# Gate and up products of a SwiGLU encoder on one core: plain tile products against 2x2x2 block products with seven multiplications, with one pool of 4 KB buffers

## The chip, the core and the metric

The kernel runs on one core of a Trainium2 chip. A core has a matrix engine (TensorE, PE in the profile; PEld is its weight loading), VectorE (DVE), ScalarE (ACT), GpSimd (POOL) and SyncE (SP), which here only issues DMA transfers. Each engine works through its own queue in order and waits for others by semaphores. Data lie in SBUF (128 partitions); products of TensorE go to PSUM, eight banks of 128 x 512 float32. The metric is the device time of one execution in microseconds, lower is better.

## The reference

Two layers, each a half-step FFN, a mixer (two attentions and a pooling branch with gates) and a second half-step FFN. The sequence has 512 tokens, the model 1,024 features, the FFN 2,816. The part that matters:

```python
def swiglu(h, w_gate, w_up, w_down):
    return (jax.nn.silu(h @ w_gate) * (h @ w_up)) @ w_down

for l in range(DEPTH):                       # DEPTH = 2
    mod = (c_act @ w_ada[l] + b_ada[l]).reshape(B, N_MOD, D_MODEL)
    h = modulate(rms_norm(x, norm_gain[l, 0]), mod[:, 0], mod[:, 1])
    x = x + 0.5 * mod[:, 2][:, None, :] * swiglu(h, ffn_w_gate[l, 0], ffn_w_up[l, 0], ffn_w_down[l, 0])
    h = modulate(rms_norm(x, norm_gain[l, 1]), mod[:, 3], mod[:, 4])
    x = x + mod[:, 5][:, None, :] * hybrid_mixer(h, ...)
    h = modulate(rms_norm(x, norm_gain[l, 2]), mod[:, 6], mod[:, 7])
    x = x + 0.5 * mod[:, 8][:, None, :] * swiglu(h, ffn_w_gate[l, 1], ffn_w_up[l, 1], ffn_w_down[l, 1])
```

All is float32.

## The kernel before

**Products in two parts.** Activations lie transposed, features on the partitions and the 512 tokens along the free side. Every large operand is kept as a high part rounded to the fast float32 format of TensorE and a low part, the rest. A product then is three matmuls, high by high, low by high and high by low, which accumulate in one PSUM bank (`triple`, L117). Weights come from DRAM in chunks of 128 x 1,024 (4 KB a partition): `wchunk` (L237) issues the load on SyncE into a `raw` buffer, ScalarE copies the high part into `whi` (L262), VectorE subtracts for the low part into `wlo` (L264); while the attentions run GpSimd does that subtraction.

**An FFN** (`Ffn.run`, L459) has 22 feature tiles of 128, in two parts of 12 and 10 tiles. For each tile a gate chunk and an up chunk of eight 128 x 128 blocks are loaded, each is multiplied by h (`hhi`, `hlo`: eight blocks of 128 x 512) in 24 matmuls of 512 columns (`unit`, L445), and `act` (L450) makes SiLU on ScalarE, the product on VectorE and the split in two parts. After a part `k_outer` (L373) multiplies by the down weights, chunk by chunk, into four banks for each half of the 1,024 model features, and `residual_tail` (L413) adds the result to x on VectorE. In the last pass of an FFN, and of the mixer, `k_outer` works in two halves of 256 tokens.

**Between the phases** the next phase's norm is prepared: `Norm.sq` (L299) squares x on ScalarE and adds on GpSimd into `ssum`, and scales x; `Norm.front` (L319) brings the sum to TensorE and VectorE works out the inverse root; `Norm.back` (L333) broadcasts it by a matmul (L345) and works through eight pieces (`piece`, L350): a multiplication on VectorE or GpSimd (`ON_DVE`, L427), the shift and the high part on ScalarE (L358), the low part on VectorE (L359). The two halves of the tokens go one after the other, and the first three units of an FFN are multiplied half by half behind them. Their weights were loaded ahead (`prefetch_weights`, L442) into spare buffers.

**Beside it** 144 vectors of the modulation are worked out (`mod_step`, L190: a load of 512 KB and one multiply-and-sum on VectorE, L196); 128 of them wait in a queue, and `wchunk` takes one for every chunk while an FFN runs and the queue lasts.

**Order.** The program is written with small delayed tasks (`later`, `poll`, counted in units of TensorE's work), and a scheduler then fixes the order on each engine and the buffers. Buffers are named by tags with a count each: `raw` 2, `whi` and `wlo` 3 each, `b` 17, `ptb` 2 of 8 KB, `pta` 1, `v2` and `xv` 4 each; PSUM has four banks named `mm` and four named `acc`.

Of the kernel before, what the change touches and what calls it, by code (L numbers as in the profile page):

```python
# [15 lines left out]
F32 = mybir.dt.float32  # L16
F32R = mybir.dt.float32r
# [12 lines left out]
H = 8  # L30
# [10 lines left out]
def encoder_kernel(tc, xT, c, w_ada, b_ada, gains, w_gate, w_up, w_down, w_qkv, w_f, w_ubg,  # L41
# [16 lines left out]
    NB, NRAW = 17, 2  # L58
# [14 lines left out]
    def blk(tag, dt=F32R):  # L73
        bufs = {"xv": 4, "v2": 4, "b": NB}[tag]
        return st([P, 2, T], dt, tag, bufs)
# [93 lines left out]
    hhi = cp.tile([P, KD, T], F32R, name="hhi")  # L169
    hlo = cp.tile([P, KD, T], F32R, name="hlo")  # L170
# [19 lines left out]
    def mod_step(l, j, d, tag="raw"):  # L190
        raw = st([P, D], F32, tag, {"v2": 4, "raw": NRAW}[tag])
# [28 lines left out]
    MOD_RATE = 1.0  # L220
# [16 lines left out]
    def wchunk(src, shape, side=True, spare=None, lo_eng=None):  # L237
        if lo_eng is None:
            lo_share[1] += 1
            lo_eng = nc.gpsimd if lo_share[0] and lo_share[1] % lo_share[0] == 0 else nc.vector  # L240
# [4 lines left out]
        elif side and in_ffn[0] and mod_tag[0] == "v2":  # L245
            mod_credit[0] += MOD_RATE
            while mod_credit[0] >= 1.0:
                mod_credit[0] -= 1.0
                mod_pop()
        raw = st([P] + list(shape), F32, "raw", NRAW)  # L250
        last["dma"] = nc.sync.dma_start(raw, src).ins
        if spare == "ptb":
            both = st([P, 2] + list(shape), F32R, "ptb", 2)
            hi, lo = both[:, 0], both[:, 1]
        elif spare == "b":
            hi = st([P] + list(shape), F32R, "b", NB)
            lo = st([P] + list(shape), F32R, "b", NB)
        else:
            hi = st([P] + list(shape), F32R, "whi", 3)
            lo = st([P] + list(shape), F32R, "wlo", 3)  # L260
        with behind("scalar"):
            nc.scalar.copy(hi, raw)  # L262
        with behind("vector"):
            lo_eng.tensor_tensor(lo, raw, hi.bitcast(F32), op=ALU.subtract)  # L264
# [23 lines left out]
    class Norm:  # L288


        def __init__(self, l, s, xtag):
            self.l, self.s, self.xtag = l, s, xtag
            self.ssum = st([P, T], F32, "ssum", 1)
# [5 lines left out]
        def sq(self, d, hs):  # L299
# [4 lines left out]
            if d == 0:  # L304
                nc.scalar.activation(self.ssum[:, cols], x, AF.Square)
# [32 lines left out]
        def back_start(self, hs, bank):  # L338
# [10 lines left out]

            def piece(d):  # L350
# [4 lines left out]
                else:  # L355
                    nc.gpsimd.tensor_tensor(t, rbs, t, op=ALU.mult)  # L356
                hi = hhi[:, d, cols]
                a_ins = nc.scalar.activation(hi, t, AF.Identity, bias=b)  # L358
                v_ins = nc.vector.scalar_tensor_tensor(hlo[:, d, cols], t, b, hi.bitcast(F32),  # L359
                                                       op0=ALU.add, op1=ALU.subtract)  # L360
# [724 lines left out]
```

## Time and profile before

| | |
|---|---|
| median of three runs | 2508.5 us (2507.54 to 2511.23) |
| the profiled execution, its own time | 2514.29 us |
| span of its profile | 2512.5 us |
| TensorE busy | 2440.8 us, 11,898 matmuls |
| VectorE, ScalarE, GpSimd busy | 1374.1, 979.7, 384.8 us |
| read from DRAM | 311.64 MB |

The profile is of one execution. Busy times of TensorE overlap, as matmuls are pipelined, so the distance from one start to the next is the better measure of their price. A group gives an instruction's line, engine, operation, tiles (out<-in) and shape, with count, busy time and mean nanoseconds, and after the second bar the engine's idle time before it and what ended that. A window gives the busy time of each engine in a stretch of time, with the number of its instructions in brackets, the granted clock of TensorE (1.00 is full), the mean share of the DMA engines and GB/s. A row of the timeline gives start, duration, engine, line, operation, tiles, shape and count.

### The profile page before, as it was taken

The page shows a single profiled execution, that of the slowest core. Times are in us where ns is not written, and L with a number is a line of the kernel's source. Part 1 is how long each engine was busy: PE and PEld are TensorE (multiplying, and loading weights), DVE is VectorE, ACT ScalarE, POOL GpSimd, SP SyncE. Part 2 cuts the span into 40 slices and gives each one's busy share as a digit, 9 for nine tenths or more (in the row PEclk, how much of TensorE's full clock was granted, in tenths as well). Part 3 has the DMA queues.
Part 4 walks back from the last instruction along what each step waited for, and adds up shares of the span by engine and source line. Part 5 has one row for each costly group of instructions (what it writes and reads, how often), then busy time and mean ns, then how long its engine had stood idle before and what let it go on. Part 6 is the DMA issues. An engine that isn't in the chain of part 4 may idle for free. (4 is left out here: it accounts for less than half of the span.)

```text
span 2512.5 us, 30820 instructions
## 1 busy us (share of the span) xinstructions
PE 2440.8 (97%) x11898; PEld 2039.0 (81%) x11898; DVE 1374.1 (55%) x2429; ACT 979.7 (39%) x1632; POOL 384.8 (15%) x369
## 2 busy tenths in 40 slices
PE   6999999999999999999999999999899999999999
PEld 5888888777788888888888888877778888888888
DVE  8655536688753365555365543367787434533332
ACT  4322235767532343222332223355766334422231
POOL 2000003243322220000020000123332322100000
PEclk9999999999999999999999999999999999999999
DMA  7655533222323335555335532323233233222322
GB/s 252 227 188 198 191 111 110 76 80 91 107 89 109 119 113 196 185 201 184 101 117 187 192 121 97 118 84 93 64 110 102 92 116 121 74 95 98 97 96 93
DMA packets 116263, 320.02 MB, mean 127 GB/s; under 512 B 11122, under 2 KB 13298, under 8 KB 116116
## 3 DMA queue, kind: packets, MB, share of 16 engines
q1 hardware_dynamic: 116114, 318.05, 37.6%
q8 instruction: 93, 1.52, 0.2%
q14 instruction: 54, 0.44, 0.1%
q10 hardware_dynamic: 2, 0.00, 0.0%
HBM read 311.64 MB, written 6.38 MB: 127 GB/s over the span
## 5 line engine op out<-in xcount | busy, mean ns | idle before, releaser
L262 ACT CAST whi<-raw 128x1024 fp32r<-128x1024 f32 (+1 forms) x395 | 411.7, 1045 | 1096.9 <-PE acc L120 421.5
L264 DVE TENSOR_TENSOR wlo<-raw,whi 128x1024 fp32r<-128x1024 f32 x339 | 419.0, 1238 | 532.2 <-ACT whi L262 520.1
L120 PE MATMUL mm<-hlo,whi 128*128 128x512 f32 x1304 | 507.8, 389 | 0.0
L121 PE MATMUL mm<-hhi,wlo 128*128 128x512 f32 x1304 | 507.7, 389 | 0.0
L119 PE MATMUL mm<-hhi,whi 128*128 128x512 f32 x1304 | 507.6, 389 | 0.0
L119 PE MATMUL acc<-b,whi 128*128 128x512 f32 (+1 forms) x960 | 359.0, 374 | 0.0
L121 PE MATMUL acc<-b,wlo 128*128 128x512 f32 (+1 forms) x960 | 357.2, 372 | 0.0
L120 PE MATMUL acc<-b,whi 128*128 128x512 f32 (+1 forms) x960 | 356.6, 372 | 0.0
L121 PEld LDWEIGHTS mm<-hhi,wlo 128*128 128x128 f32 x1304 | 245.0, 188 | 51.0
L119 PEld LDWEIGHTS mm<-hhi,whi 128*128 128x128 f32 x1304 | 245.0, 188 | 51.0
L120 PEld LDWEIGHTS mm<-hlo,whi 128*128 128x128 f32 x1304 | 245.0, 188 | 50.7
L309 POOL TENSOR_TENSOR ssum<-ssum,t 128x256 f32<-128x256 f32 (+1 forms) x45 | 53.6, 1190 | 1082.4 <-ACT t L308 1082.4
L121 PEld LDWEIGHTS acc<-b,wlo 128*128 128x128 f32 x960 | 184.6, 192 | 29.8
L120 PEld LDWEIGHTS acc<-b,whi 128*128 128x128 f32 x960 | 184.5, 192 | 29.1 <-DVE b L370 0.3
L119 PEld LDWEIGHTS acc<-b,whi 128*128 128x128 f32 x960 | 184.6, 192 | 28.9
L196 DVE CUSTOM_DVE_ANT_0 v<-v,b,badac 128x1024 f32<-128x1024 f32 x144 | 183.8, 1279 | 35.5 <-DMA v<-in_w_ada_dram 35.4
L119 PE MATMUL acc<-hhi,whi 128*128 128x512 f32 x480 | 192.0, 401 | 3.2 <-ACT hhi L555 3.2
L121 PE MATMUL acc<-hhi,wlo 128*128 128x512 f32 x480 | 190.1, 396 | 3.3 <-POOL wlo L264 3.1
L120 PE MATMUL acc<-hlo,whi 128*128 128x512 f32 x480 | 189.4, 395 | 1.5 <-DVE hlo L557 1.5
L454 DVE TENSOR_TENSOR t<-mm,t 128x512 f32<-128x512 f32 x86 | 59.4, 691 | 212.7 <-PE mm L121 208.6
L264 POOL TENSOR_TENSOR wlo<-raw,whi 128x1024 fp32r<-128x1024 f32 (+1 forms) x56 | 133.6, 2389 | 175.3 <-ACT whi L262 145.8
L119 PE MATMUL acc<-whi,hhi 128*128 128x512 f32 x336 | 138.2, 411 | 4.9 <-ACT t L642 3.7
(233 smaller groups left out, 3552.9 us busy)
## 6 DMA issues: line engine op xcount, KB each, us to landing
v<-in_w_ada_dram SPq DMA_DIRECT2D x144, 512.0 KB, 4.4
raw<-in_w_down_dram SPq DMA_DIRECT2D x88, 512.0 KB, 3.7
raw<-in_w_gate_dram SPq DMA_DIRECT2D x85, 512.0 KB, 3.4
raw<-in_w_up_dram SPq DMA_DIRECT2D x85, 512.0 KB, 3.4
raw<-in_w_ubg_dram SPq DMA_DIRECT2D x56, 512.0 KB, 3.5
raw<-in_w_qkv_dram SPq DMA_DIRECT2D x48, 512.0 KB, 3.7
raw<-in_w_branch_dram SPq DMA_DIRECT2D x24, 512.0 KB, 3.7
raw<-in_w_out_dram SPq DMA_DIRECT2D x16, 512.0 KB, 3.7
```

The source lines that it names most:

```text
L119: mm(o, lh, rh, start=start, stop=False)
L120: mm(o, lh, rl, start=False, stop=False)
L121: mm(o, ll, rh, start=False, stop=stop)
L196: nc.vector.tensor_tensor_reduce(out=raw, in0=raw, in1=silc[0], scale=1.0, scalar=badac[:, l, j, d:d + 1], op0=ALU.mult, op1=ALU.add, accu ...
L262: nc.scalar.copy(hi, raw)
L264: lo_eng.tensor_tensor(lo, raw, hi.bitcast(F32), op=ALU.subtract)
L309: nc.gpsimd.tensor_tensor(self.ssum[:, cols], self.ssum[:, cols], q, op=ALU.add)
L454: nc.vector.tensor_tensor(pr, pu, sg, op=ALU.mult)
```

## The change

The gate and up products of two feature tiles form one unit (`Unit`). The 2 x 2 blocks of a unit are two feature tiles by two halves of the 1,024 inner features for the weights (A11 to A22), and two halves of the inner features by two halves of the tokens for h (B11 to B22). Instead of eight block products there are seven, of sums of blocks (Strassen's scheme in Winograd's form): S1 to S4 are sums of weight blocks, T1 to T4 sums of blocks of h. Each of the seven is four inner blocks by three matmuls of 256 columns, 84 matmuls a unit where two tiles took 48 of 512 columns.

- The sums of the weights are made on GpSimd for each unit (`left_sums`, four operations), before the split in high and low part; the split now has three and a half chunks a unit instead of two.
- The sums of h are made once for each FFN (`combinations`, on VectorE, GpSimd and ScalarE), behind the second half of the norm. h as a whole is kept for the mixer alone, in buffers of the common pool (`hh`, `hl`).
- `combine` adds the seven results out of PSUM, on VectorE and ScalarE; the product of gate and up goes to GpSimd (`finish`).
- The first three units of an FFN (`first_units`) take products 1 and 2 behind the first half of the norm, the other five behind the second.
- An FFN has parts of 4, 6, 6 and 6 tiles, so x gets four additions instead of two. x goes to DRAM at the start of an FFN and comes back after the first part, and its buffers hold weights meanwhile.
- The first FFN takes its first four tiles as before and makes the sums behind them.
- A unit takes one `mod_step` from the queue, a chunk of the down weights two.
- One pool `b` of 23 buffers of 4 KB (it was 17 beside the 32 KB of h), `raw` 4, `pt` 4 in place of `ptb` and `pta`, `r3` 2 of 2 KB. The mixer takes its buffers from these.

The order that the scheduler makes changes with it on all engines. The diff, cut to what the text speaks of:

```diff
-    NB, NRAW = 17, 2
+    NB, NRAW = 23, 4
+    BUFS = {"xv": 4, "v2": 4, "b": NB, "raw": NRAW, "pt": 4, "whi": 3, "wlo": 3, "r3": 2}
...
+    def side_work(rate):
...
+            mod_credit[0] += rate
...
+    def wchunk(src, shape, side=True, spare=None, lo_eng=None, rate=2.0):
...
     class Norm:
...
+            def put(d):
+                if self.s == 1:
...
+                    return hh(d, cols), hl(d, cols)
+                if hs and d < 4:
+                    return None
+                return [z[:, d % 4, :] for z in self.op(("B11", "B21")[d // 4] if hs == 0 else "B22")]
...
+            if hs and self.s != 1:
+                extra = self.combinations()
+                todo[4:4] = extra[:2]
+                todo += extra[2:]
...
+        def combinations(self):
...
+            def first(q):
+                t = quarter(0, 0, q)
+                nc.vector.tensor_tensor(t, quarter(0, 1, q), t, op=ALU.subtract)
+                split("T1", q, t)
+            def second(q):
+                t12, t22, t21 = quarter(0, 1, q), quarter(1, 1, q), quarter(1, 0, q)
+                nc.gpsimd.tensor_tensor(t12, t22, t12, op=ALU.subtract)
+                nc.vector.tensor_tensor(t22, t22, quarter(0, 0, q), op=ALU.subtract)
+                nc.gpsimd.tensor_tensor(t21, t21, t22, op=ALU.subtract)
+                add(t22, shift[:, 4 + 2 * q:6 + 2 * q])
+                split("T2", q, t22)
...
+    SEVEN = {1: ("A11", "B11", ("a", 0)), 2: ("A12", "B21", ("b", 0)), 6: ("S2", "T2", ("b", 1)),
+             5: ("S1", "T1", ("c", 0)), 7: ("S3", "T3", ("c", 1)), 4: ("A22", "T4", ("d", 1)),
+             3: ("S4", "B22", ("d", 0))}
+    SPLITS = (("A11", "A12"), ("S2", "S1"), ("S3", "A22"), ("S4",))
+    class Unit:
...
+        def load(self):
+            side_work(1.0)
...
+            self.raw = [slot((2, 4, P), "raw", F32) for _ in range(2)]
...
+        def left_sums(self):
+            r1, r2 = self.raw
+            sm, s4 = slot((2, 4, P), "pt", F32), slot((4, P), "r3", F32)
+            tt = nc.gpsimd.tensor_tensor
+            tt(sm[:, 1], r2[:, 0], r2[:, 1], op=ALU.add)
+            tt(sm[:, 0], sm[:, 1], r1[:, 0], op=ALU.subtract)
+            tt(r2[:, 0], r1[:, 0], r2[:, 0], op=ALU.subtract)
+            tt(s4, r1[:, 1], sm[:, 0], op=ALU.subtract)
...
+        def product(self, i):
...
+            for k in range(4):
+                bh, bl = self.ffn.norm.b_op(right, k)
+                triple(o, wh[:, k, :], wl[:, k, :], bh, bl, k == 0, k == 3)
+            self.done.add(i)
+            self.combine()
...
+            if due(1) and not (self.lazy and len(self.done) < 3):
...
+                nc.scalar.copy(self.out[:, 1, :], self.sums.pop("a"))
+            if due(1, 2, 6):
...
+                add(self.out[:, 0::3, :], self.sums.pop("b"), twice(self.out[:, 1, :]), op=ALU.add)
...
+                add(o[:, 1:3, :], c, twice(o[:, 3, :]), op=ALU.add)
+                add(o[:, 3, :], c[:, 1, :], o[:, 1, :], op=ALU.add)
...
+                add(o[:, 1:3, :], self.sums.pop("d"), o[:, 1:3, :], op=ALU.add)
+                self.finish()
...
+            nc.gpsimd.tensor_tensor(o, o, ffn.gates.pop(self.n), op=ALU.mult)
+            hi, lo = blk("b"), blk("b")
+            split_to(hi, lo, o.rearrange("p (a b) t -> p a (b t)", a=2))
...
+            self.pre = [Unit(self, which, 0, ("b", None, "xv", "pt")) for which in range(2)]
+            for u in self.pre:
+                u.split(0)
...
+        def first_units(self):
+            g0, u0 = self.pre
+            g1 = Unit(self, 0, 2, lazy=True)
+            self.norm.back(0, mmt)
+            later(FRONT1, lambda: self.norm.front(1, mmt))
+            later(BACK1, lambda: self.norm.back(1, mmt))
+            for u, i in ((g1, 0), (g0, 3), (u0, 3), (g0, 1), (u0, 1), (g0, 2), (u0, 2)):
+                u.split(i)
...
+            for u in (g0, u0, g1):
+                u.product(1)
+                u.product(2)
+                if u is g0:
+                    for b in range(4):
+                        nc.sync.dma_start(x_dram[b], x_blocks[b].rearrange("p a t -> p (a t)"))
+            self.norm.back(1, mmt)
+            gate.clear()
+            for u, i in ((g0, 3), (u0, 3), (g0, 5), (u0, 5), (g0, 6), (u0, 6), (g0, 7), (g0, 4), (u0, 7), (u0, 4)):
+                u.product(i)
+            for i in (6, 5, 7, 4, 3):
+                g1.product(i)
...
-            for part, (f0, nf) in enumerate(((0, 12), (12, 10))):
+            parts = (4, 6, 6, 6)
...
+                for n, which in todo:
+                    u = Unit(self, which, n)
+                    for i in (1, 2, 6, 5, 7, 4, 3):
+                        u.product(i)
```

More of the change, by code (lines that the diff above doesn't have):

```diff
@@ L661, in turn @@
             if is_q:
-                lows.append(blk("b"))
+                lows.append([slot((T,), "r3") for _ in range(2)] if p == 0 else
+                            [z[:, o, :] for z in (blk("raw" if p == 1 else "b"),) for o in range(2)])
             first, second = slice(0, HD), slice(HD, P)
```

307 lines of the change are left out of this document (205 added, 102 removed).

## The prediction

> **What bounds the kernel now.** First the engine totals and the chain of waits, on the page.
>
> ```profile
> PE 2440.8 (97%) x11898; PEld 2039.0 (81%) x11898; DVE 1374.1 (55%) x2429; ACT 979.7 (39%) x1632; POOL 384.8 (15%) x369
> PE 21%; DMA 0%; issue 0%; DVE 0%; ACT 0%; POOL 0%; POOLq 0%; DVEq 0%
> ```
>
> TensorE is busy 97% of the span and the chain names nothing else of weight, so the price of a matmul decides. Busy times overlap, so I read the distance from start to start in the timeline of TensorE: two 512-column products of a gate unit, then two 256-column products where a `k_outer` ends in halves.
>
> ```profile
> 299.94 0.39 PE L119 MATMUL mm<-hhi,whi 128*128 128x512 f32 x1
> 300.17 0.39 PE L120 MATMUL mm<-hlo,whi 128*128 128x512 f32 x1
> 900.48 0.28 PE L120 MATMUL acc<-b,whi 128*128 128x256 f32 x1
> 900.60 0.28 PE L121 MATMUL acc<-b,wlo 128*128 128x256 f32 x1
> ```
>
> A 512-column matmul comes every 0.227 us (0.23 in the rows; 266 of them fill the 60.00 us below, 0.2256 each), a 256-column one every 0.120: 6% dearer than half. Next the busy times by stage, in a stretch of pure gate and up work, inside an FFN, and at the start of one.
>
> ```profile
> 60.00:120.00 60.00, 60.00 (x266) 49.43 (x265) 42.39 (x64) 21.32 (x28) 0.07 (x1) 1.00 0.65 231
> 912.00:1240.00 328.00, 327.57 (x1490) 273.07 (x1491) 178.39 (x253) 95.72 (x121) 6.09 (x6) 1.00 0.49 172
> 1240.00:1280.00 40.00, 37.35 (x291) 36.60 (x290) 21.18 (x54) 15.33 (x31) 11.40 (x13) 0.96 0.28 93
> ```
>
> The columns are PE, PEld, DVE, ACT, POOL, the granted clock and the DMA. Inside an FFN TensorE loses nothing, VectorE is busy 54%, and GpSimd idles (6.09 of 328 us). At a start (here 1240 to 1280) TensorE stands 2.65 us.
>
> **The change part by part.** *Fewer columns.* Counted over the loops, 3,624 matmuls of 512 columns go and 6,240 of 256 come (84 units of 7 products of 12; part of the split tails of the down product turn back into 512). 3,624 x 0.227 = 822.6; 6,240 x 0.120 = 748.8: **-74 us**. A unit of two feature tiles takes 84 x 0.120 = 10.1 us, where the same work took 48 x 0.227 = 10.9.
>
> *What a unit asks of the others.* The groups by line and shape give the prices:
>
> ```profile
> L264 DVE TENSOR_TENSOR wlo<-raw,whi 128x1024 fp32r<-128x1024 f32 x339 | 419.0, 1238 | 532.2 <-ACT whi L262 520.1
> L262 ACT CAST whi<-raw 128x1024 fp32r<-128x1024 f32 x387 | 405.2, 1050 | 1096.9 <-PE acc L120 421.5 <-PE mm L120 354.0 <-issue 262.1
> L196 DVE CUSTOM_DVE_ANT_0 v<-v,b,badac 128x1024 f32<-128x1024 f32 x144 | 183.8, 1279 | 35.5 <-DMA v<-in_w_ada_dram 35.4
> L264 POOL TENSOR_TENSOR wlo<-raw,whi 128x1024 fp32r<-128x1024 f32 x48 | 116.0, 2421 | 134.4 <-ACT whi L262 108.1 <-PE acc L119 17.8 <-issue 8.3
> L370 DVE TENSOR_TENSOR b<-t,b 128x512 fp32r<-128x512 f32 x88 | 60.1, 684 | 0.7 <-ACT b L369 0.7
> L454 DVE TENSOR_TENSOR t<-mm,t 128x512 f32<-128x512 f32 x86 | 59.4, 691 | 212.7 <-PE mm L121 208.6
> L369 ACT CAST b<-t 128x512 fp32r<-128x512 f32 x88 | 54.9, 626 | 1.3 <-DVE t L454 1.3
> L452 ACT ACTIVATE t<-mm 128x512 f32<-128x512 f32 x86 | 51.1, 594 | 3.3 <-PE mm L121 3.3
> L417 DVE SCALAR_TENSOR_TENSOR xv<-acc,modc,xv 128x512 f32<-128x512 f32 x56 | 41.9, 749 | 58.4 <-PE acc L121 58.4
> L356 POOL TENSOR_TENSOR v<-strip,v 128x256 f32<-128x256 f32 x30 | 24.9, 859 | 13.8 <-ACT strip L347 13.8
> ```
>
> GpSimd: four weight sums of 512, 1.29 us each (the row at 1982.07 below), and for every second unit a product of 1,024 at 2.42: 5.2 + 1.2 = 6.4 us. VectorE: three splits at 1.24, one of 512 at 0.68, four combinations out of PSUM (three at 0.69, one of half that) 2.4, half a split of the activations 0.6, and 1.28 where a `mod_step` goes along: 7.4, or 8.7. ScalarE: 3 x 1.05 + 0.63, an evacuation of 0.3, half a SiLU (0.6) and half a split (0.5), 5.2. Each is under 10.1 us and hides behind the products, if they run side by side. Two stretches of the trace say whether VectorE and GpSimd do:
>
> ```profile
> 804.46 1.23 DVE L264 TENSOR_TENSOR wlo<-raw,whi 128x1024 fp32r<-128x1024 f32 x1
> 804.51 2.33 POOL L965 TENSOR_TENSOR xv<-xv,t 128x512 f32<-128x512 f32 x1 [6.91 <-DVE t L964]
> 1982.07 1.29 POOL L965 TENSOR_TENSOR xv<-xv,t 128x512 f32<-128x512 f32 x1 [5.06 <-DVE t L964]
> 1982.08 2.37 DVE L264 TENSOR_TENSOR wlo<-raw,whi 128x1024 fp32r<-128x1024 f32 x1
> ```
>
> Whichever starts second takes its own time plus the other's: 1.29 becomes 2.33, 1.23 becomes 2.37. So operations with both inputs in SBUF exclude GpSimd's. [...]
>
> For a part of six tiles I add what excludes each other: VectorE 6 x (3.7 + 0.7 + 0.6) + 6 down chunks x 1.24 = 37.3 us, GpSimd 6 x 6.4 = 38.3, and 18 `mod_step` (one a unit, two a chunk) x 1.28 = 23. That is 75.6 us without them and 98.6 with, against 6 x 10.1 + 144 x 0.227 = 93 of TensorE. In the new instruction order the queued `mod_step` fill two parts of the first FFN, two and a half of the second and one of the third: 5.5 x 5.4 = **+30** (0 where the weights made one unit ahead cover it, 60 at double, since two queues in order don't interleave perfectly). The other parts have 18 us to spare.
>
> *The start of an FFN* (three times). The old one, in order of time on DVE, ACT and POOL:
>
> ```profile
> 898.41 0.37 ACT L347 COPY strip<-mm 128x256 f32<-128x256 f32 x1 [1.21 <-PE mm L345]
> 898.82 1.09 DVE L354 TENSOR_TENSOR b<-mm,b 128x256 f32<-128x256 f32 x3 [0.35 <-ACT strip L347]
> 903.81 0.93 POOL L309 TENSOR_TENSOR ssum<-ssum,t 128x256 f32<-128x256 f32 x1
> 905.67 0.47 DVE L359 SCALAR_TENSOR_TENSOR hlo<-b,modc,hhi 128x256 fp32r<-128x256 f32 x1
> 906.44 0.16 DVE L328 TENSOR_SCALAR nt_v<-acc 128x2 f32<-128x2 f32 x1 [0.30 <-PE acc L326]
> 908.61 0.48 DVE L331 TENSOR_SCALAR strip<-ident,nt_z 128x128 f32<-128x128 f32 x2
> 910.33 4.16 POOL L356 TENSOR_TENSOR b<-strip,b 128x256 f32<-128x256 f32 x5 [5.59 <-ACT strip L347]
> raw<-in_w_up_dram SPq DMA_DIRECT2D x85, 512.0 KB, 3.4
> ```
>
> Taking 898.0 as zero (the broadcast of the first half), the first half is modulated at 8, and GpSimd starts the second at 12. In the new instruction order both queues hold weight work between the halves. On VectorE: five splits of 1,024 and two of 512 (7.6 us) stand ahead of the statistics of half two. On GpSimd: the sums of g1 and then of u1 stand ahead of its five multiplications, and u1's second weight tile can only be loaded once the split into `xv` has freed its buffer. So: VectorE at 8 + 6.5 = 14.5 (18 where the four sums of g1, 5.2 us, take turns); the load 3.4: 18 to 21.5; four sums 5.2: 23 to 27; two multiplications 1.7; then the first combination, 0.7 + 0.63 + 0.68: T1 stands at 27 to 31. TensorE has until then 24 tail matmuls and six products: 96 x 0.120 = 11.5 us. It waits 15 to 19, then some 3 for T2 (0 to 6). Less the 2.65 of now: 17 each, **+51** (36 to 66).
>
> The statistics of half one wait for GpSimd too: sums of u0 stand between the `ssum` additions, about two operations: 3 x 2.5 = **+7.5** (0 to 15).
>
> A stall has a second price, seen where TensorE stood once:
>
> ```profile
> 386.55 0.28 PE L120 MATMUL acc<-b,whi 128*128 128x256 f32 x1
> 388.35 0.69 PE L326 MATMUL mm<-ones,strip 128*128 128x1 f32 x4 [1.52 <-DVE strip L314]
> 389.47 0.41 PE L120 MATMUL acc<-b,whi 128*128 128x256 f32 x1
> 389.69 0.41 PE L121 MATMUL acc<-b,wlo 128*128 128x256 f32 x1
> 392.21 0.28 PE L121 MATMUL acc<-b,wlo 128*128 128x256 f32 x1
> ```
>
> For 3.4 us the matmuls come every 0.213 instead of 0.120: 16 x 0.093 = 1.5 us. It is paid at the starts today too, so it adds nothing there. [...]
>
> *The rest.* After the four-tile part the down product needs the last unit's activations: 0.69 + 2.42 + 1.05 + 1.24 = 5.4 us behind 24 matmuls of 5.4; a sum in between makes 1.5, three times **+4.5** (0 to 12). The extra residual tails (64 x 0.75 = 48 us) lie on VectorE's idle time in the down product; without that cover they would delay the reuse of PSUM. x's trip to DRAM is DMA, which is half idle. The third copy of each of the eight blocks of x at the very start, **+3** (0 to 5). The 4 KB pool leaves the mixers as many buffers as they had: 0 (-10 to 10), for the reordering only.
>
> Sum: -74 + 30 + 51 + 7.5 + 4.5 + 3 = **+22 us**. The profiled execution took 2514.3 us (span 2512.5 and 1.8 around it), 5.8 above the median of 2508.5; the difference goes on the median: **2531 us**.
>
> **The rivals.** *A: the side work hides, and the change pays.* For it: VectorE is 54% busy and GpSimd idle in the old FFN, and a unit's splits are made one unit ahead. Against: the exclusion rows. Starts at their lower bound, no turns taken: 36; the lock nothing; the rest 0: -74 + 36 = -38, **2470**. *B: the lock binds every unit.* In series VectorE (6.3, or 5.0) and GpSimd (6.4) need 12.7 us a unit with a `mod_step` and 11.4 without, from the point where this exceeds 10.1 for longer than the run-ahead of some 4 us a part. 52 units (18, 22 and 12 of the first three FFNs) x 2.6 + 32 x 1.3 = 177, less 15 parts x 4 = 60: 117 in place of 30, **2618**. Against it: the down products let both engines catch up. *C: the change doesn't do what it says,* because a 256-column product isn't half of a 512 one: its weight load is busy longer than the 0.120:
>
> ```profile
> L119 PEld LDWEIGHTS acc<-b,whi 128*128 128x128 f32 x960 | 184.6, 192 | 28.9
> ```
>
> At 0.136 the gain is gone: 6,240 x 0.016 = 100, **2631**. Against it: the rows at 900 load weights for every matmul and keep 0.120.
>
> **How the numbers follow.** The forecast has 0.50 (own range 2505 to 2560), A 0.30, B 0.14, C 0.06. 0.2% is 5 us, what a measurement can tell from no change. Faster: A and the lower end of the forecast, 0.33. Same: 0.06. Slower: 0.61. The range runs from A, a little widened, to the middle between forecast and B: 2462 to 2592.
>
> **What would show it.** Right: 256-column products 0.120 apart inside units; at three places, after the second broadcast, TensorE idle 15 to 19 us with GpSimd at weight sums of u1; GpSimd's 512-element operations well above 1.29 us in the mean, and gaps in the units of the first three FFNs but not the last. Wrong: starts under 8 us, or no gaps in loaded parts (A); units above 11 us everywhere (B); products more than 0.13 apart (C).

## The result, and the profile after

The changed kernel takes 2842.6 us (median of 4 runs, 2840.3 to 2846.2) where the kernel before takes 2509.1 on the same chip (4 runs): a ratio of 1.133, 95% interval 1.131 to 1.135. It is 333 us slower. The prediction said 2531, with a range from 2462 to 2592.

Where the time lies can be read from the first broadcast of each norm (`mm(rb, ...)`, line 345 before and 359 after), which starts once in every phase. The distances between these starts, in us (the first FFN counts from the start of the trace, the last one up to the start of TensorE's last matmul):

```
phase            FFN 1   mixer 1   FFN 2   FFN 3   mixer 2   FFN 4
before           393.8     504.0   369.7   371.0     502.6   367.8
after            448.3     546.7   443.3   426.4     549.4   422.4
difference       +54.5     +42.7   +73.6   +55.4     +46.8   +54.6
```

Every phase lost. The FFNs, which should have gained 15 to 18 us each by their columns, lost 238 in all, and the mixers, whose arithmetic is as it was, lost 89. First the page of the profile after: the engine totals, and three groups.

```profile
PE 2497.9 (88%) x14514; PEld 2176.9 (77%) x14514; DVE 1835.5 (65%) x2911; ACT 1150.7 (41%) x1864; POOL 1066.4 (38%) x763
...
L573 ACT CAST pt<-r 128x512 fp32r<-128x512 f32 x84 | 51.8, 621 | 553.6 <-POOL r L554 506.4
...
L626 POOL TENSOR_TENSOR b<-b,b 128x1024 f32<-128x1024 f32 x42 | 108.8, 2591 | 331.0 <-DVE b L617 261.2
...
L552 POOL TENSOR_TENSOR pt<-pt,raw 128x512 f32<-128x512 f32 x84 | 156.9, 1868 | 6.3
```

TensorE fell from 97% to 88% of a longer span. No other engine is full: VectorE has 65%, GpSimd 38%. Yet ScalarE stood 553.6 us at the head of one small group, the split of S4, and 506.4 of these it waited for GpSimd's last sum. That is the line to follow. Next the stretches of the second FFN and of the last one, first after, then before; the columns are the engines' busy times, then granted clock, DMA share and GB/s.

```profile
995.00:1438.00 443.00, 373.08 (x2460) 341.46 (x2459) 334.69 (x438) 153.56 (x210) 206.57 (x123) 0.94 0.43 148
...
2414.00:2840.00 426.00, 372.28 (x2483) 343.46 (x2481) 234.72 (x290) 143.38 (x189) 163.55 (x107) 0.94 0.26 87
```

```profile
898.00:1267.00 369.00, 365.54 (x1785) 310.12 (x1784) 200.95 (x308) 111.32 (x152) 18.43 (x18) 1.00 0.47 163
...
2141.00:2512.00 371.00, 367.10 (x1810) 311.66 (x1809) 133.55 (x166) 100.56 (x133) 10.61 (x13) 1.00 0.28 93
```

The last FFN has no `mod_step` at all, so the prediction gave it no gaps but at its start. It stands 426 - 372 = 54 us, and its 2,483 matmuls (456 of 512 columns, nearly all others of 256: 456 x 0.227 + 2,027 x 0.120 = 347 us) keep TensorE busy for 372, because the clock is at 0.94 in the mean. So two things were lost: TensorE waited, and it then ran slowly. In the whole trace the halved clock lasts 292 us, where before it lasted 27. By the totals on the two pages TensorE stands 2840 - 2498 = 342 us, where it stood 72: the waits grew by 271. Its busy time grew by 57, though the columns by their number alone should have taken 74 off, so running slowly cost some 131, an estimate from these totals.

What TensorE waits for, from the view of waits (us in total, times, longest):

```profile
PE mm L126 <- DVE wlo L275: 64.0, 60, 3.3
PE mm L124 <- ACT whi L273: 36.1, 32, 3.7
PE mm L359 <- DVE strip L345: 30.4, 3, 10.1
PE mm L124 <- ACT b L429: 23.9, 3, 8.2
PE mm L340 <- DVE strip L328: 19.9, 3, 7.4
PE acc L124 <- ACT whi L273: 19.3, 11, 5.7
PE acc L126 <- DVE wlo L275: 17.6, 14, 2.4
PE acc L126 <- POOL wlo L275: 15.9, 11, 1.7
PE acc L124 <- ACT b L460: 15.4, 7, 3.7
PE acc L124 <- DVE xv L508: 14.2, 6, 4.8
```

Three kinds stand here. The waits for `whi` and `wlo` by `mm` banks are inside the units: weights not yet split at products 1 or 7 (product 6, which goes to an `acc` bank, waits as well, some 17 us in all). Those at lines 359, 340 and `ACT b L429` come three times each and belong to the starts of three FFNs, 74 us together; the one at 340, for the statistics of half one, lies just ahead of the first broadcast. `POOL wlo` is the mixers' own weight split on GpSimd, for which the kernel before waited 3.1 us in all.

**One unit in close view.** The trace shows 75 units whole. They last 12.3 us in the mean, where 84 products of 0.120 make 10.1: some 167 us over. Take the one whose first product starts at 2640.2, in the last FFN. The timeline of its second half and of what feeds it, all engines in order of time (columns: start, duration, engine, line):

```profile
2634.76 1.23 DVE L275 TENSOR_TENSOR wlo<-raw,whi 128x1024 fp32r<-128x1024 f32 x1
...
2636.01 0.33 SPq L541 DMA_DIRECT2D raw<-in_w_up_dram  x1
...
2639.48 1.81 POOL L551 TENSOR_TENSOR pt<-raw 128x512 f32<-128x512 f32 x1 [6.35 <-DMA raw<-in_w_up_dram]
...
2641.37 2.16 POOL L552 TENSOR_TENSOR pt<-pt,raw 128x512 f32<-128x512 f32 x1
...
2643.49 1.28 POOL L553 TENSOR_TENSOR raw<-raw,raw 128x512 f32<-128x512 f32 x1
...
2644.74 1.28 POOL L554 TENSOR_TENSOR r<-raw,pt 128x512 f32<-128x512 f32 x1
...
2646.05 0.62 ACT L573 CAST pt<-r 128x512 fp32r<-128x512 f32 x1 [6.21 <-POOL r L554]
...
2646.58 1.04 ACT L273 CAST whi<-raw 128x1024 fp32r<-128x1024 f32 x1
...
2646.70 0.69 DVE L575 TENSOR_TENSOR pt<-r,pt 128x512 fp32r<-128x512 f32 x1 [3.72 <-ACT pt L573]
...
2647.65 1.23 DVE L275 TENSOR_TENSOR wlo<-raw,whi 128x1024 fp32r<-128x1024 f32 x1
...
2647.67 0.39 PE L124 MATMUL mm<-b,whi 128*128 128x256 f32 x1 [1.55 <-ACT whi L273]
...
2648.93 0.39 PE L126 MATMUL mm<-b,wlo 128*128 128x256 f32 x1 [0.76 <-DVE wlo L275]
...
2652.44 1.29 POOL L551 TENSOR_TENSOR pt<-raw 128x512 f32<-128x512 f32 x1 [0.45 <-DMA raw<-in_w_gate_dram]
```

The sums from 2639.48 on belong to the *next* unit, whose S4 is needed some 20 us after it is ready (2646.0), in its last product (2666.05). But in the instruction order the split of that S4 (lines 573 and 575) stands ahead of the *running* unit's split of S3 and A22 (lines 273 and 275 from `raw`). ScalarE waits 6.21 us at the head of its queue for GpSimd, VectorE 3.72 for ScalarE, and the weights for product 7, whose buffer has been loaded for long, come late: TensorE stands 1.55 and 0.76. Now look at the first and the last rows. The load of 2636.01 was issued as the split from `raw` before it ended at 2635.99, because that split frees the buffer. So the chain closes on itself: split of S3 and A22, load (3.4 us), four sums (6.5), split of S4 (1.3), split of S3 and A22. From first sum to first sum it takes 2652.44 - 2639.48 = 13.0 us, and while it is closed, units follow each other no faster than its turns, however idle each engine is.

### The profile page after: what moved, and what is told of

It reads as the page before. It is cut to its first block, busy times and chain, and to the rows that moved or that the text cites. A ratio compares the mean times of both kernels' runs of the same rounds, so it can differ in the third digit from the quotient of the medians.

```text
span 2840.2 us, 37869 instructions
## 1 busy us (share of the span) xinstructions
PE 2497.9 (88%) x14514; PEld 2176.9 (77%) x14514; DVE 1835.5 (65%) x2911; ACT 1150.7 (41%) x1864; POOL 1066.4 (38%) x763
## 3 DMA queue, kind: packets, MB, share of 16 engines
q8 instruction: 114, 1.87, 0.3%
## 5 line engine op out<-in xcount | busy, mean ns | idle before, releaser
L124 PE MATMUL acc<-b,whi 128*128 128x512 f32 (+1 forms) x2400 | 846.2, 354 | 49.8 <-ACT b L460 15.4
L126 PE MATMUL acc<-b,wlo 128*128 128x512 f32 (+1 forms) x2400 | 839.8, 350 | 33.8 <-DVE wlo L275 17.6
L125 PE MATMUL acc<-b,whi 128*128 128x512 f32 (+1 forms) x2400 | 837.6, 349 | 9.6 <-DVE b L461 4.7
L124 PEld LDWEIGHTS acc<-b,whi 128*128 128x128 f32 x2400 | 469.8, 196 | 112.6 <-DVE xv L508 19.1
L126 PEld LDWEIGHTS acc<-b,wlo 128*128 128x128 f32 x2400 | 468.9, 195 | 97.6 <-DVE wlo L275 24.7
L125 PEld LDWEIGHTS acc<-b,whi 128*128 128x128 f32 x2400 | 470.3, 196 | 63.5 <-DVE b L461 9.6
L126 PE MATMUL mm<-b,wlo 128*128 128x256 f32 (+1 forms) x1120 | 337.7, 302 | 64.1 <-DVE wlo L275 64.0
L124 PE MATMUL mm<-b,whi 128*128 128x256 f32 (+1 forms) x1120 | 334.1, 299 | 60.2 <-ACT whi L273 36.1
L125 PE MATMUL mm<-b,whi 128*128 128x256 f32 (+1 forms) x1120 | 329.9, 295 | 0.7 <-DVE b L430 0.7
L551 POOL TENSOR_TENSOR pt<-raw 128x512 f32<-128x512 f32 x84 | 124.1, 1477 | 544.8 <-DMA raw<-in_w_up_dram 276.3
L126 PEld LDWEIGHTS mm<-b,wlo 128*128 128x128 f32 x1120 | 223.1, 199 | 79.1 <-DVE wlo L275 77.3
L124 PEld LDWEIGHTS mm<-b,whi 128*128 128x128 f32 x1120 | 222.5, 199 | 73.4 <-ACT whi L273 44.2
L573 ACT CAST pt<-r 128x512 fp32r<-128x512 f32 x84 | 51.8, 621 | 553.6 <-POOL r L554 506.4
L125 PEld LDWEIGHTS mm<-b,whi 128*128 128x128 f32 x1120 | 222.3, 199 | 3.7 <-DVE b L430 1.6
L552 POOL TENSOR_TENSOR pt<-pt,raw 128x512 f32<-128x512 f32 x84 | 156.9, 1868 | 6.3
L124 PE MATMUL acc<-whi,b 128*128 128x512 f32 x336 | 139.4, 422 | 9.4 <-ACT whi L273 6.4
```

What stands on the lines that cost most here:

```text
L124: mm(o, lh, rh, start=start, stop=False)
L125: mm(o, lh, rl, start=False, stop=False)
L126: mm(o, ll, rh, start=False, stop=stop)
L551: tt(sm[:, 1], r2[:, 0], r2[:, 1], op=ALU.add)
L552: tt(sm[:, 0], sm[:, 1], r1[:, 0], op=ALU.subtract)
L573: nc.scalar.copy(z[:, 0], s4)
```

## The experiments

Times are medians on the chip, each beside runs of the kernel before (2509 to 2511 us); ratios are to that kernel, with 95% intervals. The recorded expectations use short names: e1_s4_order is the kernel of the first experiment, e3_plain_pool the one with plain products in the new pool, e10_dve_pta the three edits together, e13_plain_start the plain start on top of these, e14 the one with no `mod_step` beside the units and e16_half_rate the one with one for every second unit. By the lock they, and the rivals of the prediction, mean the exclusion of VectorE and GpSimd in the prediction's rows at 804.46 and 1982.07 (1.29 us became 2.33, 1.23 became 2.37). At the start of an FFN g0 and u0 are the first gate and up unit, g1 and u1 the second.

**Order of the splits.** The split of S4 is queued behind the unit's own split of S3 and A22 on each of the two engines; `follows` sets the place in the queue and waits for nothing:

```
-                with behind("scalar"):
+                with follows("scalar", late[0]):       # ScalarE's copy of S3, A22
                     nc.scalar.copy(z[:, 0], s4)
-                with behind("vector"):
+                with follows("vector", late[1]):       # VectorE's low part of S3, A22
                     nc.vector.tensor_tensor(z[:, 1], s4, ...)
```

> Theory (a loop through the queues): the split of S4 of the next unit stands ahead of the split of S3 and A22 of the running unit on ScalarE and VectorE, and waits for the last of GpSimd's sums; those wait for a load, whose buffer only the split of S3 and A22 frees. Once round: load 3.4 us, four sums 5.2 to 7, S4 1.3, split 2, some 13 us a unit. Here each unit's S4 split is queued behind its own split of S3 and A22, nothing else changes. The loop is open then: the stalls at product 7 (44.6 us in the 75 units that the trace shows whole) and most at product 1 (52 us) go, with the halved clock behind each; units of 12.3 us in the mean come to 10.3 to 10.8; 2842 falls to 2690 to 2740. Rival (the lock and the load on GpSimd and VectorE set the pace, the order doesn't): under 30 us, 2815 to 2845.

Measured: 2716.8 us, 1.083 (1.080 to 1.086), 126 less. The stalls at product 7 fell from 44.6 to 5.1 us, those at product 1 only from 52.0 to 31.2; units came from 12.3 to 11.0, in the last FFN to 10.3. The three rows below are VectorE in that FFN: the low part from `raw` no longer stands behind the one from `r`.

```profile
2551.76 1.26 DVE L284 TENSOR_TENSOR wlo<-raw,whi 128x1024 fp32r<-128x1024 f32 x1
2552.94 0.68 DVE L629 TENSOR_TENSOR b<-acc,b 128x512 f32<-128x512 f32 x1
2553.54 0.68 DVE L587 TENSOR_TENSOR pt<-r,pt 128x512 fp32r<-128x512 f32 x1
```

Six units of the same FFN in the view by stretches, TensorE busy for 61.06 of 62.00 us:

```profile
2520.00:2582.00 62.00, 61.06 (x502) 60.35 (x500) 46.06 (x51) 27.66 (x35) 35.67 (x18) 1.00 0.33 103
```

GpSimd's sums were no faster than before: its group means here are 1462, 1908, 2005 and 1864 ns where the changed kernel has 1477, 1868, 1741 and 1601. Where nothing stands in the way one takes 1.28 (the row at 2644.74). So VectorE and GpSimd held each other up as ever, and 126 us went by order alone.

**Without the sums.**

```
-            tt(sm[:, 1], r2[:, 0], r2[:, 1], op=ALU.add)   # and three more
+            sm, s4 = r1, r1[:, 1]
```

> The four sums of a unit's weight blocks are left out (the raw blocks stand in their place), all loads, splits and products stay. Theory of the loop: 5.2 to 7 us of 13 go from it, so units come to about 10.2 us, and at the starts of the FFNs the second half is not held up by sums: 2590 to 2640. Rival 1 (the load and its buffers alone set the pace, without the sums): units stay above 11.5, over 2760. Rival 2 (VectorE's own work, with mod_step, sets it): units of the first three FFNs stay long, those of the last do not; 2700 to 2760.

Measured: 2583.7 us, 1.030 (1.027 to 1.033). The units take 10.14 us in the mean, 5 us over in all 75, with `mod_step` beside them as before; the time is a little under the range. So the load alone doesn't set the pace, and VectorE's work without sums fits under the products.

**Plain products in the new pool.** All gate and up units as before the change, the rest of the changed kernel as it is (parts, pool, mixers).

> Gate and up by plain products again (512 columns, no sums, no combinations), with the one pool of buffers, the four parts and the rest of the changed kernel. Theory (the pool costs the mixers their 89 us, through the raw buffers that attention now shares with the weights): 2590 to 2620, mixers still 547 us. Rival (the mixers lose because of what the seven-product units leave around them): 2505 to 2530, mixers 504 us.

Measured: 2573.4 us, 1.026 (1.023 to 1.029). Mixers 539.1 and 536.9 us, FFNs 396.4, 364.6, 364.7 and 367.0; the time lies between theory and rival. The four parts and the extra residual tails cost the FFNs nothing in sum (x stays in SBUF here); the pool costs the mixers 35 us each. The 7.6 and 12.5 that the mixers lose beyond this come with the seven-product units.

**A buffer of its own for the turned probabilities.**

```
-    NB, NRAW = 23, 4
+    NB, NRAW = 22, 4                       # and a tag "pta" with 1 buffer
-                    z = slot((2, nj, 256), "raw")
+                    z = slot((2, nj, 256), "pta")
```

> The mixer's first half of turned probabilities gets a buffer of its own again instead of one of the four raw buffers; the b buffers fall from 23 to 22 for it. Theory (this sharing holds the weight loads of the mixers up): mixers from 547 to 505 to 520 us, 2842 falls to 2780 to 2800. Rival (they lose for want of b buffers, 15 where 17 were): mixers 550 to 560, 2845 to 2870.

Measured: 2789.1 us, 1.112 (1.108 to 1.116), 53 less; mixers 517.7 and 518.5. The view of waits between 450 and 970 us, the first mixer, no longer has a row for `POOL wlo`, and the longest wait left belongs to the statistics:

```profile
PE mm L340 <- DVE strip L328: 7.4, 1, 7.4
PE acc L124 <- ACT whi L273: 4.8, 1, 4.8
PE mm L1047 <- DVE pta L1029: 2.6, 2, 1.5
```

The raw buffers that attention held were missing for the weight loads, as the theory said, and one b buffer less cost nothing to be seen.

**Sums held back at the start of an FFN.** Two edits on the kernel of the first experiment (2716.8). In the first, the sums of the units loaded ahead wait for the statistics:

```
+            with after("pool"), after("ssum"):     # last GpSimd work for half one, last addition of the statistics
                 self.four_sums()
```

> The kernel of e1_s4_order (2717), and the weight sums of the two units loaded ahead of an FFN are queued on GpSimd behind the statistics of both halves and the modulation of the first. Theory (those sums stand between the additions of the statistics): the wait before the first broadcast (7.6 us, with 10 us of halved clock behind it) goes at three places: 10 to 13 us each, 30 to 40 less: 2677 to 2690. The price may come back at the second broadcast, if the sums then push the modulation of half two: 2700 to 2717. Rival (the wait is for something else): 2717 or more.

Measured: 2703.7 us, 1.077 (1.074 to 1.079), 13 less. The price came back, as the middle case said, and more than half of it: mixers 5 and 10 us shorter, but the second broadcast came 30.2 us after the first (23.1 before), FFN 3 and 4 longer by 7 and 6.

In the second, the sums of g1 and u1 wait for GpSimd's work on half two:

> The kernel of e1_s4_order, and the sums of g1 and u1 at the start of an FFN are queued on GpSimd behind its work for the second half of the activations. Theory of the prediction (sums of u1 and g1 ahead of the modulation hold the second half): the second broadcast comes 3 to 8 us earlier (23.1 us after the first now), TensorE waits 10 less at each of three starts: 2680 to 2700. Rival (the second half waits on VectorE's queue, behind the splits of the first units): the second broadcast moves by less than 2 us, 2705 to 2725.

Measured: 2711.2 us, 1.080 (1.078 to 1.082), 6 less, where its three runs lie 8 apart; in the rival's range. The second broadcast did come 5.2 us earlier (17.9), yet TensorE gained next to nothing: in the start of FFN 2 its wait for the statistics fell from 8.9 to 3.6 us, and others, up to 2.9 for a combination on VectorE, came in its place. So GpSimd's queue did hold the second half up, against the rival, but what it held up wasn't all that the products wait for.

**A short `mod_step`.**

```
-  nc.vector.tensor_tensor_reduce(out=raw, in0=raw, in1=silc[0], ...)
+  nc.vector.tensor_tensor_reduce(out=raw[:, :8], in0=raw[:, :8], in1=silc[0][:, :8], ...)
```

> The kernel of e1_s4_order, and the reduction of mod_step runs over 8 of its 1,024 columns; its loads stay. Theory (mod_step fills the room that the lock leaves): the first FFN, 429.8 us from start to broadcast, and the second, 419.2, lose 25 to 40 each, the third 5 to 10, the last (381.4) nothing: 2640 to 2660. Rival (the remaining gaps are order alone): each FFN within 5 us, 2700 to 2720.

Measured: 2668.9 us, 1.063 (1.060 to 1.065), 48 less. FFN 1 became 21 us shorter, FFN 2 16, FFN 3 10, and FFN 4 stayed (381.4 and 381.0): the right places, two thirds of the size.

**Sums on VectorE.** Four operations of 0.68 us in place of four of 1.28 on GpSimd, with the new order of S4 and without it:

```
-            tt = nc.gpsimd.tensor_tensor
+            tt = nc.vector.tensor_tensor
```

> The kernel of e1_s4_order with the four weight sums of a unit on VectorE instead of GpSimd (0.68 us each instead of 1.28). Theory (GpSimd's slowness and the lock make the remaining gaps in the units): VectorE has 7.4 + 2.7 = 10.1 us a unit, 11.4 with a mod_step, and takes no turns any more but for one product a pair: 2670 to 2710, the last FFN 365 to 380. Rival (VectorE becomes the bound): units of 11 or more everywhere, 2730 to 2800.

Measured: 2635.6 us, 1.049 (1.047 to 1.051); the last FFN 369.4 us, with units of 10.1. The time is better than the theory gave, the last FFN as it said.

> The changed kernel with the weight sums on VectorE, and without the new place of the split of S4. Theory (the loop is made by the order of the queues, and the slow sums on GpSimd only set how long it is): four sums in 2.7 instead of 5.2 to 7 us shorten the loop from 13 to about 9 to 10 us, under the 10.1 of the products, so most of it goes even in the old order: 2640 to 2700. Rival (the order alone decides, whoever sums): 2740 to 2800, units still above 11.5.

Measured: 2637.6 us, 1.051 (1.046 to 1.057). So the four cells are 2842.6 (old order, GpSimd), 2716.8 (new order), 2637.6 (VectorE), 2635.6 (both). Once the sums are fast the order of S4 no longer matters, as the theory has it; and the sums on GpSimd cost 81 us even in the good order, for which the loop alone doesn't account. The two traces with the new order say where these lie: the 75 whole units are 67 us over their 10.08 with GpSimd and 10 with VectorE, and the waits for the statistics at three starts of FFNs fall from 20.2 to 3.8 us (first half) and from 26.7 to 19.9 (second half). Six units of the last FFN with the old order and sums on VectorE:

```profile
2434.00:2494.00 60.00, 60.00 (x502) 59.86 (x501) 49.73 (x63) 27.78 (x34) 6.54 (x2) 1.00 0.31 98
```

TensorE loses nothing with VectorE at 83% of the stretch and GpSimd at 11. Four sums that took GpSimd 6.7 us in the mean (1.48 + 1.87 + 1.74 + 1.60 in the changed kernel) take VectorE 3.1 in this kernel (0.73 + 0.72 + 0.74 + 0.86), and 0.68 each where nothing stands in the way.

**Three together, and a new order at the start.**

> Three edits together: S4 behind S3 and A22, sums on VectorE (2636 with these two), and a buffer of its own for the mixer's turned probabilities (53 less on the changed kernel). If the causes lie apart, their gains add up: 2575 to 2590. Rival (with shorter FFNs the buffers of the mixers no longer matter, or one b buffer less costs the units): 2600 or more.

Measured: 2578.7 us, 1.027 (1.025 to 1.029). The gains add up. Then u0's later splits were queued behind the statistics of half two, and the sums of g1 and u1 behind its modulation:

```
-            for u, i in ((g1, 0), (g0, 3), (u0, 3), (g0, 1), (u0, 1), (g0, 2), (u0, 2)):
+            for u, i in ((g0, 2), (g1, 0), (g0, 3), (u0, 3), (g0, 1)):   # u0's 1 and 2 after front(1)
```

> The kernel of e10_dve_pta, and at the start of an FFN the splits of u0's later blocks are queued behind the statistics of the second half, the sums of g1 and u1 behind the modulation of the second half. Theory (the second half waits in VectorE's queue): the second broadcast comes 11 to 14 us after the first instead of 20.8, TensorE waits 7 to 10 less at each of three starts and the halved clock shortens with it: 25 to 45 less than e10_dve_pta, 2535 to 2560. Rival (the splits are then late for the products that follow): 0 to 10 less or more.

Measured: 2593.3 us, 1.033 (1.031 to 1.035), 15 *more*. The second broadcast moved from 20.8 to 15.6 us, and the wait before it from 6.6 to 1.4; but what had been moved came late for later products, and in the last FFN TensorE stood 16.6 us in all (15.1 before). The theory of one queue fell. Of three new orders at the start two gained 13 and 6 us and one lost 15, which fits more side work there than six products hide, so that order only chooses where TensorE waits; that reading is argued, not shown.

The same buffer for the probabilities, in the kernel with plain products:

> The kernel of e3_plain_pool (2573) with the buffer of its own for the turned probabilities. Theory (sharing the raw buffers is what the pool costs): mixers 539 to about 510, 2510 to 2525. Rival (b buffers, 14 for the mixers where 17 were): 2540 or more.

Measured: 2516.7 us, 1.003 (1.002 to 1.004); mixers 510.7. The sharing of the raw buffers was 57 of the 64 us that the pool cost. The last 7 to 8 a mixer are open: 14 b buffers for 17, or the order, were not told apart.

**A plain start.** Every FFN makes its four-tile part by plain products, and T1 to T4 beside them:

```
-            g0, u0 = self.pre
-            g1 = Unit(self, 0, 2, lazy=True)
...
+            g0, u0, g1 = self.pre                  # plain weights, both halves as in the kernel before
...
+            for f in self.norm.combinations():     # behind the fourth tile
+                f()
```

> The kernel of e10_dve_pta (2579), and every FFN begins as the first one does: its four-tile part by plain products, the combinations T1 to T4 made beside them, x not sent to DRAM. This gives back 512-column products for 4 of 22 tiles in three FFNs (3 x 4 x 0.8 = 10 us). Theory (the start of an FFN by seven products costs some 25 us, the statistics of half one 8): three starts 75, five to eight in each mixer: 2579 + 10 - 75 - 14: 2490 to 2520. Rival (the combinations beside the plain products delay these as much): 2560 or more.

Measured: 2531.9 us, 1.009 (1.007 to 1.011), 47 less than 2578.7, above the theory's range and under the rival's. The last FFN takes 352.8 us, 15.0 *less* than the 367.8 of the kernel before: 18 units with 0.8 us less each make 14.4. Here the fewer columns pay in full, TensorE busy for 352.31 of 356 us:

```profile
2174.00:2530.00 356.00, 352.31 (x2413) 328.40 (x2411) 266.26 (x347) 143.58 (x190) 43.01 (x26) 1.00 0.30 94
```

FFN 2 and 3, with `mod_step` beside their units, are at 371.5 and 370.9, FFN 1 at 410.3.

The same start on the changed kernel:

> The changed kernel with the plain start alone; order, sums and pool as they were. Theory (prediction's terms for the start, +51, the statistics, +7.5, and the halved clock on top of them, measured as some 30 us at each of three places): 2843 + 10 - 90 - 15: 2735 to 2765. By the prediction's own terms, 58 less 10: 2790 to 2800. Rival (the units take up what the start leaves, since their loop sets the pace anyway): 2820 or more.

Measured: 2747.5 us, 1.096 (1.094 to 1.097), 95 less with 10 given back by the columns: the starts and the statistics cost the changed kernel some 105 us, while its units still stall as they did (12.3 us each). Some 7 of the 105 are the stalls of three whole units that became plain.

**Where `mod_step` goes.** None beside the units (side work 0 a unit, 2 with each plain weight):

> The kernel of e13_plain_start, and no mod_step goes along with a seven-product unit; two go along with each plain gate or up weight and each down chunk. Theory (with 10.1 us of VectorE work a unit has no room for 1.28 more): the first three FFNs lose 10 to 20 each: 25 to 50 less than e13, 2450 to 2485, under the 2509 of before. Rival (the mod_steps stretch the down products instead): within 10 of e13.

Measured: 2530.4 us, 1.009 (1.007 to 1.011): as 2531.9, and the rival's outcome (25 to 50 less than 2532 would have been 2482 to 2507, not the 2450 to 2485 of the expectation). FFN 1 fell from 410.3 to 400.8, FFN 3 rose from 370.9 to 379.5: it has 40 `mod_step` in place of 20, FFN 1 56 in place of 74. One for every second unit:

> The kernel of e13_plain_start (2532) with one mod_step for every second seven-product unit instead of one each; two with each down chunk and one with each plain weight as before. Theory (VectorE has no room beside the units for all, and too little beside the down products for those of e14): the second and third FFN, 371 us, lose 5 to 12 each, the first some 5: 2505 to 2522. Rival (the sum of VectorE's work over the FFN decides, wherever it is put): 2525 to 2535.

Measured: 2522.5 us, 1.006 (1.004 to 1.008), 9 less, between theory and rival, and from FFN 1 (398.9, with 65 `mod_step`) and the mixers; FFN 2 and 3 stayed at 372, where 5 to 12 less each were expected. FFN 3 had 31 `mod_step` in place of 20, so a gain by their place can have been used up there. Whether the sum of VectorE's work decides or its place isn't shown by this run.

On top of this, two edits at once:

> The kernel of e16_half_rate; the first of the four weight sums goes back to GpSimd (9.4 us of VectorE a unit), and the first FFN makes its combinations T1 to T4 behind its fourth tile instead of ahead of the activations of the first three. Theory: the gaps of the first FFN between 56 and 73 us (some 8 us, and as much for the halved clock) shrink by 8 to 14, the units of the first three FFNs gain 5 to 10 in all: 2490 to 2510, at or under the kernel before. Rival (one sum on GpSimd brings the turns with VectorE back): 2520 or more.

Measured: 2537.7 us, 1.012 (1.010 to 1.014), 15 more than without these two edits, which weren't tried one by one. (In the changed kernel the first FFN makes its sums of h behind the products of three tiles, ahead of the fourth.) The weights of the first FFN's down product now stood behind the moved combinations and the `mod_step`s in VectorE's queue, and TensorE waited 10.4 us for one of them; FFN 2 and 3 rose by 3 and 5 us. None of the kernels with seven products beats the one before; the nearest, with a `mod_step` for every second unit, is 0.6% slower.

## Why the prediction was wrong, point by point

**The price of a column: right.** 256-column products came 0.120 us apart in the units; an undisturbed unit took 10.1 us; and where nothing else was in the way the gain arrived, 15.0 us in the last FFN of the plain start. Rival C is out.

**A unit hides behind its products: this step failed.** The prediction added up each engine's busy time, found each under 10.1 us, and put a price only where the sum of the excluding operations passed TensorE's time: "the other parts have 18 us to spare". Spare time in a sum is of no use to a chain that waits in queues. The chain ran over four engines and a load and came back to its own buffer; its length was 13 us, though beside TensorE no engine was busy for more than about 7 us a unit (VectorE 42.5 us in a stretch of 73 with six units). The new instruction order, in which the split of the next S4 stands ahead of the split that frees the buffer, lay before the prediction and was read for what it moves at the starts, not for what waits behind what within a unit. Price: 126 us by order alone, 205 with the sums moved to VectorE.

Rival B comes near the length of a unit (12.7 or 11.4, measured 12.3), and for another reason: with the exclusion of VectorE and GpSimd and the sums as they were, a new place for one small split brought the last FFN's units to 10.3. Its sign, units above 11 us everywhere, came true (12.2 to 12.6 in the mean of each FFN); the forecast's own sign, gaps in the first three FFNs but not the last, did not. The exclusion was a part of it all the same, since it stretched GpSimd's sums from 1.28 us to means of 1.5 to 1.9 and the loop with them. The row below, from the kernel with the sums on VectorE, shows it at work the other way round: an addition of 0.68 us next to GpSimd's product of gate and up (3.22 us there; two of them take 6.54 between 2434 and 2494) takes 2.89.

```profile
2455.58 2.89 DVE L554 TENSOR_TENSOR r<-raw,pt 128x512 f32<-128x512 f32 x1
```

**+30 for `mod_step`: right in place, too small.** 48 us went with it from the first three FFNs and none from the last, inside the bound of 60.

**+51 for the starts: right in the waits, too small by the clock behind them.** T1's products began 33 us after the first broadcast (27 to 31 predicted; the 6.5 us of splits in that sum are 7.6 by the prediction's own count). VectorE and TensorE in one start:

```profile
1008.02 4.52 DVE L275 TENSOR_TENSOR xv<-raw,xv 128x1024 fp32r<-128x1024 f32 x2
...
1012.46 0.15 DVE L342 TENSOR_SCALAR nt_v<-mm 128x2 f32<-128x2 f32 x1
1012.57 2.17 DVE L275 TENSOR_TENSOR wlo<-pt,whi 128x1024 fp32r<-128x1024 f32 x1
...
1014.66 1.22 DVE L281 TENSOR_SCALAR nt_j<-nt_v 128x2 int32<-128x2 int32 x1
...
1019.53 1.19 PE L359 MATMUL mm<-strip,ones 128*128 128x256 f32 x2 [10.13 <-DVE strip L345]
...
1028.59 1.40 PE L124 MATMUL mm<-b,whi 128*128 128x256 f32 x3 [7.86 <-ACT b L429]
```

The statistics of half two stood behind u0's splits, as the prediction said, and TensorE waited 10.1, 7.9 and 2.1 us, 20 where 15 to 19 and 3 were forecast. What was mis-sized is the term beside it: of the halved clock the prediction said that it "adds nothing there", since it is paid at the starts of the old kernel too. There it lasted 3.4 us. Here, with three waits close together, it lasted from 1014.2 to 1038.1, 23.9 us, and the 256-column matmuls in between came every 0.213 us instead of 0.120.

**+7.5 for the statistics of half one: right in mechanism, too small.** TensorE waited 19.9 us in three places, before the halved clock. Together with the starts: 58 forecast, 105 measured by the plain start on the changed kernel, 57 on the kernel whose loop was gone.

**Mixers 0: failed.** "The 4 KB pool leaves the mixers as many buffers as they had" counted b buffers and left out that the turned probabilities, which had a buffer of their own, now take raw ones from the weight loads. 53 to 57 us by three comparisons; the statistics' wait lies in the mixers' phases too, which the plain start on the changed kernel made 13 and 15 us shorter, and some 7 to 8 each stay open.

**Residual tails on idle time: right where the cover held.** In the changed kernel TensorE waited 14.2 us for them in six places; in the first experiment, with VectorE's queue no longer blocked, 1.1 in two. The +4.5 at the end of the four-tile part, 1.5 at each of three places, is too small: TensorE waits 3.7, 3.6 and 2.9 us there for the last activations (`ACT b L460`), each time with a halved stretch beside it. The +3 of the first FFN wasn't tried by itself.

**The range.** Its upper end is said to be the middle between the forecast and B. That is 2575, not 2592; the measured time is above both.

The undoing in steps, each from the one before: 2842.6; sums on VectorE and S4 in order 2635.6; the probabilities' own buffer 2578.7; a plain start 2531.9; a `mod_step` for every second unit 2522.5. That is 320 of 333 us.

## What to carry to other kernels

Busy times under the bound don't make a stage safe: follow one item of each kind through the queues, note at each step what stands ahead of it in order and which buffer its end frees, and add up the chain until it comes back to its start. A look-ahead operation that waits for a slow engine must stand behind the work that is needed sooner; and when buffers are pooled, count who held one of his own before. A saving of 3% in TensorE's columns is small against the stalls that its side work can cause, each of which may be paid a second time in clock.

## What the runs showed of the hardware that was not expected

In this case's traces the halved clock goes by a grid: in the clock records of all 19 (before, after and the experiments) the halved stretches begin at multiples of 3.4133 us from one another, within 0.01 us, and last 3.4 us or a multiple. The table counts waits of TensorE, taken from the start of one matmul of 128 columns or more to the start of the next, with the clock full at their beginning and no other wait of 0.9 us within 7 us. So often a halved stretch began during the wait or in the 3.5 us behind it:

```
0.9 to 1.8 us    2 of 391
1.8 to 2.2      16 of  85
2.2 to 3.0      41 of  54
3.0 to 5.0      34 of  40
over 5.0        13 of  13
```

The stall of the prediction's rows at 386.55 and 388.35, which are 1.80 us apart, belongs in the third line: the four matmuls at 388.35 have one column each, and the next wide one starts 2.35 us after that of 386.55.

```profile
388.90 0.56 PE L121 MATMUL acc<-b,wlo 128*128 128x256 f32 x1
```

So stalls under 1.8 us that stood alone cost next to no clock here (2 of 391), while waits of 2.2 to 3.0 us were enough in 41 of 54 cases.
